# Out-projection A of a hybrid decoder step: loads issued from among the last gates, and a wait for each piece

## The chip, the cores and the metric

The kernel runs on one core of a Trainium2 chip. The metric is the device time of one execution in microseconds (us), as the median of several runs; lower is better. TensorE multiplies matrices, VectorE (DVE), ScalarE (ACT) and GpSimd (POOL) do the element-wise work, and SyncE (SP) issues the DMA transfers between device memory (DRAM) and the on-chip memory. TensorE's results go to PSUM banks, from which another engine evacuates them. Each engine takes its instructions in the order in which the program has them, and an instruction that waits holds up all behind it on that engine.

## The reference

One inference step of a decoder with two layers, for a prompt of 1024 positions (`x_prompt`) and 8 samples of one position each (`x_sample`), model width 1024, all in 32-bit floats. The part that the change touches is layer A, a gated-DeltaNet layer:

```python
def gdn_layer(x, conv_buf, s0, norm_g, w_in, conv_w, a_log, dt_bias, o_norm, w_out):
    proj = rmsnorm(x, norm_g) @ w_in
    qkv, gate, a, beta_logit = jnp.split(proj, [...], axis=-1)
    qkv, new_buf = causal_conv_silu(qkv, conv_buf, conv_w)
    ...
    o, s_fin = gated_delta_rule(q, k, v, g, beta, s0)
    o = rmsnorm(o, o_norm) * jax.nn.silu(gate)
    y = o.reshape(b, L, GDN_V_W) @ w_out
    return x + y, new_buf, s_fin
```

There are 8 heads of width 128; `gated_delta_rule` works through chunks of 64 positions, with a triangular inverse in each and a state that goes from chunk to chunk. The last matrix product, `o @ w_out` with a 1024 x 1024 matrix, plus the residual `x`, is out-projection A. Layer B (windowed attention with its own projections) follows and reads the sum.

## The kernel before, in words

Matrix operands are split into a high and a low part (`F32R` tiles; ScalarE copies the high part, VectorE subtracts it from the original for the low part), and a product is three matmuls: high by high, high by low, low by high (`PRS`, L1281). A weight or an input therefore goes from DRAM into a `raw` tile, and from there through one ScalarE cast and one VectorE subtraction into its high and low halves.

The kernel has three stretches. Up to about 81 us it loads and normalizes the input and does the first projections. Then comes the planned stage, which is about half of the span: the rest of layer A with most of its out-projection. Last comes the ordinary program (from L1392 on): the out-projection of the last two heads and of the samples, and layer B.

**The planner.** In the planned stage the work is written as generators (L599 to L1376) that yield operations instead of issuing them. The class `Order` (L478) keeps an estimated clock for each engine, the estimated time at which each part of each tile is ready, and a priority for each generator; `run` (L566) always emits the operation that can start first by these estimates. A generator can also yield `need(...)`, which lets it go on when other generators have set certain marks, and `get(...)`, which takes one of a counted set of slots (`od.slots`: PSUM tiles). `need` and `get` act at planning time only: they decide at which place of the order an operation is put. On the chip the engines wait for each other by semaphores on the data. All operations of the stage are issued from one line, L542, so in the profile they all carry that line. The constant `D0` (L53, used at L594) is the estimated time at which the decay inputs (`ghi`, `glo`, `eG` and others) are ready.

The generators that matter here:

- `proj_all` (L738), of the lowest priority (`FILL`, 9), yields the projections of layer A's input, head by head: k, q, v and gate of each head, in three groups of positions (384, 384, 264; `GRP`), 24 matmuls each. The gates of the last two heads (`late`) come at the very end (L763), group by group. Being of the lowest priority, these matmuls fill the gaps between the recurrence (`chains`), the inverses (`inverse`) and their preparation. The input that they read lies in the tiles `xg0` and `xg1` of the pool `wide` (tag `A`, two buffers) and `xg2` of the pool `thr`.
- `feed` and `split_all` (L690, L701) load and split the projection weights, through the two `raw` buffers of `raw0` (`RB[0]` is 2).
- `samples` (L1270) does the state update of the 8 samples: loads of the states (`ssm`), small matmuls (`sp`), updates (`up`) and stores.
- `out_all` (L1357) is called by `proj_all` when all gates are planned. It closes the pools of the gate weights and of the convolution inputs (`es2w`), opens on their place two more raw buffers (`raw1`) and the pool `p3a` for the input tiles, takes the two buffers of `wide` for the first two weight halves (`woa0` and `woa1`: 6 of 8 heads, 512 columns each) and starts `out_loads`. Then it waits for the mark `wa` (both halves split) and, for each of the 8 tiles of 128 positions, for the mark `ol` (the tile's inputs split), and yields 2 x 18 matmuls per tile. `out_evac` (L1349) adds the residual `hx` to the result and stores the sum to `hD`.
- `out_loads` (L1297) lists what is to be loaded: twelve weight pieces of one head by 512 columns, then for each tile two input pieces (`oD`, three heads each) and, between, the weight pieces of heads 6 and 7. Its `feed2` issues the loads; before the two input pieces of a tile it loads the residual tile `hx`. Tiles `ohl` (inputs) and `hx` have two buffers each, so the load of tile t waits in the plan for the store of tile t - 2.

Of the kernel before, what the change touches and what calls it, by code (L numbers as in the profile page):

```python
# [49 lines left out]
GA = 1  # L50


D0, PEM, VF, DP = 6000.0, 250.0, 1.0, 2000  # L53


@with_exitstack
def hybrid_step(
# [420 lines left out]
    class Order:  # L478
# [7 lines left out]
        def mark(self, *tok):  # L486
            self.toks.add(tok)
# [4 lines left out]
        def spawn(self, pri, gen):  # L492
            self.procs.append([pri, gen, None, 0.0])
# [105 lines left out]
    def need(*toks):  # L599
        yield ("need", toks)  # L600

    def get(name):
        yield ("get", name)
# [164 lines left out]

# [528 lines left out]
    def out_loads(wb, p3a):  # L1297

        src = w_out_a[0].rearrange("(k p) c -> p k c", p=P)
        todo = []  # L1300
        for j in range(2):
            c_ = ts(j, 512)
            todo += [("w", wa[j][:, 0, k:k + 1], wa[j][:, 1, k:k + 1], src[:, k:k + 1, c_]) for k in range(K1)]
        for t in range(NT):
            todo += [("o", t, k) for k in range(0, K1, 3)]
            if t in (2, 3):
                c_ = ts(t - 2, 512)
                todo += [("w", wb[:, 0, k - K1:k - K1 + 1, c_], wb[:, 1, k - K1:k - K1 + 1, c_], src[:, k:k + 1, c_])
                         for k in range(K1, KT)]
        nr = RB[0] + RB[1]  # L1310
        dsts = {}

        def feed2():
            for i, it in enumerate(todo):
                if i >= nr:
                    yield from need(("split2", i - nr))
                if it[0] == "o":
                    t, k = it[1:]
                    if k == 0:
                        yield from need(("o", K1 - 1))  # L1320
                        if t >= 2:
                            yield from need(("ot", t - 2))
                        ohl = p3a.tile([P, 2, K1, P], F32R, tag="ohl", name="ohl")
                        hx = p3a.tile([P, D], F32, tag="hx", name="hx")
                        ohx[t] = (hx, ohl)
                        yield dq.dma_start(out=hx, in_=x_prompt[0, ts(t, P), :])
                    hi, lo, sr = ohx[t][1][:, 0, k:k + 3], ohx[t][1][:, 1, k:k + 3], oD[:, k:k + 3, ts(t, P)]
                else:
                    hi, lo, sr = it[1:]
                _, nk, c = sr.shape  # L1330
                raw = raws[i % nr >= RB[0]].tile([P, 512], F32, tag="raw", name="raw")[:, :nk * c]
                raw = raw.rearrange("p (k c) -> p k c", c=c)
                yield dq.dma_start(out=raw, in_=sr)
                dsts[i] = (raw, hi, lo)
                mark("raw2", i)

        spawn(1.2, feed2())
        for i, it in enumerate(todo):
            yield from need(("raw2", i))
            raw, hi, lo = dsts.pop(i)  # L1340
            yield sq.copy(hi, raw)
            yield vq.tensor_tensor(out=lo, in0=raw, in1=hi.bitcast(F32), op=ALU.subtract)
            mark("split2", i)
            if it[0] == "o" and it[2]:
                mark("ol", it[1])
            elif i == 2 * K1 - 1:
                mark("wa")

    def out_evac(t, ci, ps):  # L1349
        hx, _ = ohx[t]  # L1350
# [2 lines left out]
        if ci:  # L1353
            yield dq.dma_start(out=hD[ts(t, P), :], in_=hx)
            mark("ot", t)

    def out_all():  # L1357
        es2w.close()
        raws.append(es3a.enter_context(tc.tile_pool(name="raw1", reuse_waits="tile", bufs=RB[1], side="right")))
        wa.extend(wide.tile([P, 2, K1, 512], F32R, tag="A", name=f"woa{i}") for i in range(2))  # L1360
        wb = thr.tile([P, 2, KT - K1, D], F32R, tag="B", name="woa2")
        wb_.append(wb)
        p3a = es3a.enter_context(tc.tile_pool(name="p3a", reuse_waits="tile", bufs=2, side="right"))
        spawn(1.2, out_loads(wb, p3a))
        spawn(8, out_gains(p3a))
        yield from need(("wa",))
        for t in range(NT):
            yield from need(("ol", t))
            _, ohl = ohx[t]
            for ci in range(2):  # L1370
                yield from get("pj")
                ps = pj.tile([P, 512], F32, tag="pj", name="pj")
                for i, (a, b) in enumerate(PRS):
                    for k in range(K1):
                        yield pm(ps, ohl[:, a, k, :], wa[ci][:, b, k, :], i + k == 0, i == 2 and k == K1 - 1)
                spawn(1.5, out_evac(t, ci, ps))  # L1376

    for i in range(2):
# [479 lines left out]
```

## Time and profile before

| | |
|---|---|
| median of 3 runs | 1325.34 us (1321.8 to 1326.71) |
| the profiled execution | 1322.79 us |
| its span, first to last instruction | 1321.1 us |
| mean granted TensorE clock | 0.977 of full speed |
| TensorE matmuls, busy share of the span | 94% |
| VectorE, ScalarE, GpSimd | 70%, 48%, 22% |
| data moved by DMA | 92.03 MB, mean 70 GB/s |

How to read it: the profile is of one execution. Times count from the start of the span. PE is TensorE's matmuls, PEld its weight loads, SPq the queue that issues DMA transfers. A busy share is an average over the whole span; a stage has to be read by itself. The granted clock is 1.00 at 2.4 GHz and 0.50 at 1.2 GHz, so a stretch between has been partly at each. In a timeline row stand the start, the duration, the engine, the line, the operation, the tile it writes and the tiles it reads (buffer numbers left out), and how many instructions are merged in the row; in square brackets the idle time before, and what ended it.

### The profile page before, as it was taken

How to read it: one execution, taken by the hardware profiler on the slowest of the kernel's cores; microseconds unless marked ns; L12 is line 12 of the kernel's file. 1: busy time of each engine (PE TensorE's matmuls, PEld its weight loads, DVE VectorE, ACT ScalarE, POOL GpSimd, SP SyncE). 2: the span in 40 equal slices, each digit the busy share in tenths (PEclk: the TensorE clock that was granted, in tenths of full speed). 3: DMA queues.
4: the chain of work that ended last, by engine and by line, in shares of the span. 5: the costliest groups of instructions: out<-in, count | busy, mean ns of one | idle time of the engine just before them, and what ended most of it. 6: DMA issues, size and time to landing. Idle time of an engine off the chain costs nothing.

```text
span 1321.1 us, 24330 instructions
## 1 busy us (share of the span) xinstructions
PE 1242.1 (94%) x8887; PEld 1121.0 (85%) x8887; DVE 923.8 (70%) x2656; ACT 634.8 (48%) x1812; POOL 286.5 (22%) x404
## 2 busy tenths in 40 slices
PE   4979999999999999989989898899999999999998
PEld 3979998899998989888967676788888888888898
DVE  7467778878978887788776329767686686777221
ACT  5235545645454454546352116455575476577100
POOL 1045243423323353243301103202011020000000
PEclk9989999999999999999979899999998999999999
DMA  7021101110221222111063657302011021102332
GB/s 236 1 80 34 35 17 51 34 52 18 67 65 53 78 65 85 34 35 35 25 194 118 211 186 221 88 17 64 4 43 39 4 55 29 49 1 69 127 96 72
DMA packets 131987, 92.03 MB, mean 70 GB/s; under 512 B 33880, under 2 KB 123712, under 8 KB 131808
## 3 DMA queue, kind: packets, MB, share of 16 engines
q1 hardware_dynamic: 131868, 90.48, 23.3%
q8 instruction: 70, 1.15, 0.4%
q14 instruction: 49, 0.40, 0.1%
HBM read 69.28 MB, written 23.25 MB: 70 GB/s over the span
## 4 chain that ended last, share of the span: by engine, by line
PE 69%; DVE 19%; ACT 5%; DMA 4%; issue 3%; SPq 0%; POOL 0%; DVEq 0%; ACTq 0%; POOLq 0%
PE pj L542 24%; PE pj L99 17%; PE ivt L542 4%; PE chB L542 3%; PE sps L99 3%; DVE co L542 2%; PE op L99 2%; PE chA L542 2%; PE ptp L1641 1%; DMA out_dram<-hx 1%; DVE wqkv L81 1%; DVE fu L542 1%; PE sp L542 1%; PE tq L1588 1%; DMA raw<-oD 1%
## 5 line engine op out<-in xcount | busy, mean ns | idle before, releaser
L542 PE MATMUL pj<-xg,whi 128*128 128x384 f32 (+1 forms) x1392 | 291.9, 336 | 0.0
L542 PEld LDWEIGHTS pj<-xg,whi 128*128 128x128 f32 x1392 | 223.2, 191 | 2.0 <-issue 1.5
L99 PE MATMUL pj<-wqkv,ng 128*128 128x384 f32 x768 | 154.2, 345 | 0.0
L542 PE MATMUL pj<-xg,wlo 128*128 128x384 f32 (+1 forms) x696 | 152.2, 335 | 0.0
L542 DVE SCALAR_TENSOR_TENSOR co<-ue,cvT,co 128x528 f32<-128x528 f32 x144 | 131.0, 916 | 12.3 <-ACT co L542 10.5
L99 PEld LDWEIGHTS pj<-wqkv,ng 128*128 128x128 f32 x768 | 132.6, 190 | 5.0 <-issue 4.6
L542 PEld LDWEIGHTS pj<-xg,wlo 128*128 128x128 f32 x696 | 112.3, 190 | 1.1 <-issue 0.5
L92 POOL TENSOR_TENSOR raw<-raw,gains 128x512 f32<-128x512 f32 x40 | 44.6, 1123 | 280.0 <-DMA raw<-in_w_in_b_dram 150.8
L99 PE MATMUL pj<-wob,oh 128*128 128x384 f32 (+1 forms) x576 | 98.1, 325 | 0.0
L99 PEld LDWEIGHTS pj<-wob,oh 128*128 128x128 f32 x576 | 90.7, 191 | 1.8 <-issue 1.5
L542 PE MATMUL pj<-woa,ohl 128*128 128x512 f32 x288 | 79.8, 428 | 6.5 <-ACT ohl L542 6.5
L542 PEld LDWEIGHTS pj<-woa,ohl 128*128 128x128 f32 x288 | 56.7, 204 | 21.6 <-ACT ohl L542 7.7
L542 ACT COPY ue<-pj 128x384 f32<-128x384 f32 (+1 forms) x88 | 32.2, 376 | 51.4 <-PE pj L542 43.6
L1819 DVE TENSOR_TENSOR hx<-hx,pj 128x384 f32<-128x384 f32 (+3 forms) x27 | 13.7, 508 | 59.0 <-PE pj L99 41.6
L542 POOL TENSOR_TENSOR ue<-ue,co 128x528 f32<-128x528 f32 x24 | 36.7, 1530 | 75.4 <-ACT ue L542 75.4
L542 DVE TENSOR_TENSOR wlo<-raw,whi 128x512 fp32r<-128x512 f32 x58 | 44.5, 770 | 9.9 <-ACT whi L542 9.4
L542 ACT ACTIVATE ue<-co 128x528 f32<-128x528 f32 x48 | 31.0, 645 | 31.3 <-DVE co L542 30.9
L542 ACT CAST whi<-raw 128x512 fp32r<-128x512 f32 x58 | 35.8, 619 | 19.6 <-PE pj L542 19.5
L99 PE MATMUL op<-pt,vsb 128*64 128x256 f32 x240 | 37.9, 396 | 0.7 <-DVE e L1625 0.5
L542 POOL TENSOR_TENSOR co<-co,ue 128x528 f32<-128x528 f32 x24 | 37.7, 1570 | 1.3
L542 ACT ACTIVATE qs<-chB,eG 128x128 f32<-128x128 f32 x56 | 20.5, 366 | 35.1 <-PE chB L542 34.5
L99 PE MATMUL sps<-kTh,qst 128*128 128x256 f32 (+1 forms) x144 | 36.9, 295 | 0.0
(906 smaller groups left out, 2950.4 us busy)
## 6 DMA issues: line engine op xcount, KB each, us to landing
raw<-in_w_in_a_dram SPq DMA_DIRECT2D x64, 256.0 KB
ssm<-in_state_ssm_dram SPq DMA_DIRECT2D x32, 256.0 KB
hD<-hx SPq DMA_DIRECT2D x16, 512.0 KB
raw<-in_w_in_b_dram SPq DMA_DIRECT2D x32, 256.0 KB
xt<-in_x_prompt_dram SPq DMA_DIRECT2D x8, 512.0 KB
out_dram<-ssm SPq DMA_DIRECT2D x16, 256.0 KB
raw<-in_w_out_a_dram SPq DMA_DIRECT2D x16, 256.0 KB
hx<-in_x_prompt_dram SPq DMA_DIRECT2D x8, 512.0 KB
```

The source lines that it names most:

```text
L81: V.tensor_tensor(out=lo, in0=raw, in1=hi.bitcast(F32), op=ALU.subtract)
L92: G.tensor_tensor(out=raw, in0=raw, in1=gain[:, k:k + n].unsqueeze(2).broadcast_to([P, n, c]), op=ALU.mult)
L99: PE.matmul(out, lhsT, rhs, start=start, stop=stop, skip_group_check=True)
L542: op.f(*op.a, **op.k)
L1588: PE.transpose(tq[:, ts(h, P)], qhl[:, h].rearrange("p a d -> p (a d)"), identr)
L1641: PE.transpose(pp[:, ts(h, P)], pr[h // 2][:, h % 2, ts(kt, P)], ident)
L1819: V.tensor_tensor(out=hx[:n, :cn], in0=hx[:n, :cn], in1=ps[:n, :cn], op=ALU.add)
```

## The change

- The first weight tile, `woa0`, is taken from `wide` as soon as the gates of the first group of positions are planned, and `out_loads` is started there; the second, `woa1`, after the gates of the second group. Before, both were taken after all gates.
- The list of loads is in another order: the six pieces of the first weight half, the two input pieces of tile 0, the six pieces of the second half, and then tile by tile as before.
- The loads of the second weight half and of the inputs wait (in the plan) for the mark `out`, set by `out_all` when the pools of the gate weights are closed. Up to there two raw buffers serve the loads, then four; they are counted as slots of `od`.
- The residual tile `hx` is loaded after the second input piece of its tile, before it was loaded ahead of the first.
- The marks `wa` and `ol` are gone. Each matmul needs (in the plan) its own weight piece and its own input piece.
- `D0` goes from 6000 to 12000 (ns).

```diff
-D0, PEM, VF, DP = 6000.0, 250.0, 1.0, 2000
+D0, PEM, VF, DP = 12000.0, 250.0, 1.0, 2000
...
         for gi in range(3):
             for i, (h, _) in enumerate(late):
                 yield from gate_group_a(h, gi, w_of[n + i])
+            if gi < 2:
+                wa.append(wide.tile([P, 2, K1, 512], F32R, tag="A", name=f"woa{gi}"))
+            if gi == 0:
+                spawn(1.2, out_loads())
...
-        todo = []
-        for j in range(2):
-            c_ = ts(j, 512)
-            todo += [("w", wa[j][:, 0, k:k + 1], wa[j][:, 1, k:k + 1], src[:, k:k + 1, c_]) for k in range(K1)]
-        for t in range(NT):
+        od.slots["raw"] = RB[0]
+        todo = [("w", 0, k, ts(0, 512)) for k in range(K1)] + [("o", 0, k) for k in range(0, K1, 3)]
+        todo += [("w", 1, k, ts(1, 512)) for k in range(K1)]
+        for t in range(1, NT):
             todo += [("o", t, k) for k in range(0, K1, 3)]
             if t in (2, 3):
...
         def feed2():
+            yield from need(("split", 2 * len(jobs) - 1))
             for i, it in enumerate(todo):
-                if i >= nr:
-                    yield from need(("split2", i - nr))
                 if it[0] == "o":
                     t, k = it[1:]
                     if k == 0:
-                        yield from need(("o", K1 - 1))
+                        yield from need(("o", K1 - 1), ("out",))
                         if t >= 2:
                             yield from need(("ot", t - 2))
...
-                        yield dq.dma_start(out=hx, in_=x_prompt[0, ts(t, P), :])
...
+                    j, k, c_ = it[1:]
+                    if j:
+                        yield from need(("out",))
...
+                yield from get("raw")
+                pool = rawfree.pop(0)
...
                 yield dq.dma_start(out=raw, in_=sr)
...
+                if it[0] == "o" and it[2]:
+                    yield dq.dma_start(out=ohx[it[1]][0], in_=x_prompt[0, ts(it[1], P), :])
...
     def out_all():
         es2w.close()
...
-        spawn(1.2, out_loads(wb, p3a))
-        spawn(8, out_gains(p3a))
-        yield from need(("wa",))
+        rawfree.extend([1] * RB[1])
+        od.slots["raw"] += RB[1]
+        mark("out")
+        spawn(8, out_gains(p3a[0]))
         for t in range(NT):
-            yield from need(("ol", t))
-            _, ohl = ohx[t]
             for ci in range(2):
                 yield from get("pj")
                 ps = pj.tile([P, 512], F32, tag="pj", name="pj")
                 for i, (a, b) in enumerate(PRS):
                     for k in range(K1):
-                        yield pm(ps, ohl[:, a, k, :], wa[ci][:, b, k, :], i + k == 0, i == 2 and k == K1 - 1)
+                        yield from need(("w", ci, k), ("o", t, 3 * (k // 3)))
+                        yield pm(ps, ohx[t][1][:, a, k, :], wa[ci][:, b, k, :], i + k == 0, i == 2 and k == K1 - 1)
```

## Rows read from the trace of the kernel before

**Rows 1.** Busy times of the page: us, share of the span, instructions.

```profile
PE 1242.1 (94%) x8887; PEld 1121.0 (85%) x8887; DVE 923.8 (70%) x2656; ACT 634.8 (48%) x1812; POOL 286.5 (22%) x404
```

**Rows 2.** Stretches: from:to length, busy us of PE PEld DVE ACT POOL, clock, DMA.

```profile
81.40:89.10 7.70, 1.99 (x6) 1.00 (x5) 6.88 (x9) 5.30 (x10) 4.58 (x5) 0.78 0.26 68
89.10:664.00 574.90, 554.76 (x4714) 520.09 (x4713) 467.17 (x997) 291.24 (x876) 213.69 (x309) 0.99 0.17 47
630.00:664.00 34.00, 32.95 (x299) 31.90 (x298) 24.53 (x68) 11.41 (x41) 8.42 (x14) 0.95 0.16 45
664.00:700.40 36.40, 29.17 (x193) 24.17 (x193) 27.74 (x76) 19.23 (x54) 3.75 (x5) 0.67 0.52 157
673.10:700.40 27.30, 21.92 (x100) 17.90 (x101) 21.41 (x59) 11.97 (x32) 3.03 (x3) 0.57 0.51 154
735.70:765.70 30.00, 29.70 (x111) 22.25 (x112) 11.04 (x21) 5.18 (x12) 4.75 (x7) 0.91 0.75 234
774.30:777.10 2.80, 0.06 (x1) 0.00 (x0) 0.69 (x1) 0.51 (x2) 0.00 (x0) 1.00 0.52 202
777.10:787.20 10.10, 10.05 (x36) 8.00 (x37) 1.74 (x3) 0.49 (x2) 0.00 (x0) 0.83 0.01 5
787.20:830.00 42.80, 37.82 (x183) 26.31 (x182) 38.17 (x116) 28.61 (x49) 11.41 (x13) 1.00 0.69 206
```

**Rows 3.** Timeline of TensorE's matmuls, at the start, the hand-over and the out-projection.

```profile
87.50 0.80 PE L542 MATMUL dps<-gm,mgtr 128*128 128x512 f32 x1 [5.46 <-POOL gm L542]
...
110.99 3.07 PE L542 MATMUL pj<-xg,whi 128*128 128x384 f32 x16
...
663.25 0.49 PE L542 MATMUL pj<-xg,whi 128*128 128x264 f32 x2
...
693.19 2.05 PE L542 MATMUL pj<-woa,ohl 128*128 128x512 f32 x4
...
735.76 11.04 PE L542 MATMUL pj<-woa,ohl 128*128 128x512 f32 x36 [3.50 <-ACT ohl L542]
...
765.70 8.66 PE L542 MATMUL pj<-woa,ohl 128*128 128x512 f32 x36 [0.23 <-ACT ohl L542]
```

**Rows 4.** Timeline of the DMA queue (SP), hand-over and out-projection.

```profile
660.61 1.88 SPq L542 DMA_DIRECT2D raw<-in_w_out_a_dram  x4
...
672.03 11.22 SPq L542 DMA_DIRECT2D raw<-in_w_out_a_dram  x7
...
729.05 0.39 SPq L542 DMA_DIRECT2D out_dram<-ssm  x1
...
766.22 0.32 SPq L542 DMA_DIRECT2D hD<-hx  x1
...
770.08 0.33 SPq L542 DMA_DIRECT2D hx<-in_x_prompt_dram  x1
770.51 1.48 SPq L542 DMA_DIRECT2D raw<-oD  x2
```

**Rows 5.** Timeline of ScalarE (ACT).

```profile
81.90 1.13 ACT L542 CAST whi<-raw 128x512 fp32r<-128x512 f32 x2
...
85.78 0.57 ACT L542 ACTIVATE dt<-dps 128x512 f32<-128x512 f32 x1
...
632.23 0.49 ACT L542 ACTIVATE ogs<-pj 128x384 f32<-128x384 f32 x1
...
665.40 0.62 ACT L542 CAST woa<-raw 128x512 fp32r<-128x512 f32 x1
...
755.56 0.71 ACT L1415 CAST ohl<-ogs 128x256 fp32r<-128x256 f32 x2
```

**Rows 6.** Timeline of VectorE (DVE).

```profile
107.22 0.69 DVE L542 TENSOR_TENSOR m<-nps,dt 128x512 f32<-128x512 f32 x1
...
687.18 0.69 DVE L542 TENSOR_TENSOR woa<-raw,woa 128x512 fp32r<-128x512 f32 x1 [0.56 <-ACT woa L542]
...
727.69 0.75 DVE L542 SCALAR_TENSOR_TENSOR ogs<-otp,ogain,ogs 128x512 f32<-128x512 f32 x1
```

More of the change, by code (lines that the diff above doesn't have):

```diff
@@ L1295, in out_gains, with out_loads @@
         free("gen")
-    def out_loads(wb, p3a):
+    rawfree = [0] * RB[0]
+    def out_loads():
         src = w_out_a[0].rearrange("(k p) c -> p k c", p=P)
-        todo = []
-        for j in range(2):
-            c_ = ts(j, 512)
-            todo += [("w", wa[j][:, 0, k:k + 1], wa[j][:, 1, k:k + 1], src[:, k:k + 1, c_]) for k in range(K1)]
-        for t in range(NT):
+        od.slots["raw"] = RB[0]
+        todo = [("w", 0, k, ts(0, 512)) for k in range(K1)] + [("o", 0, k) for k in range(0, K1, 3)]
+        todo += [("w", 1, k, ts(1, 512)) for k in range(K1)]
+        for t in range(1, NT):
             todo += [("o", t, k) for k in range(0, K1, 3)]
             if t in (2, 3):
[L1307 to L1311, printed above, removed]
+                todo += [("w", 2, k, ts(t - 2, 512)) for k in range(K1, KT)]
+        pieces = {}
         def feed2():
+            yield from need(("split", 2 * len(jobs) - 1))
             for i, it in enumerate(todo):
-                if i >= nr:
-                    yield from need(("split2", i - nr))
                 if it[0] == "o":
@@ L1319, in feed2 @@
                     if k == 0:
-                        yield from need(("o", K1 - 1))
+                        yield from need(("o", K1 - 1), ("out",))
                         if t >= 2:
                             yield from need(("ot", t - 2))
-                        ohl = p3a.tile([P, 2, K1, P], F32R, tag="ohl", name="ohl")
-                        hx = p3a.tile([P, D], F32, tag="hx", name="hx")
-                        ohx[t] = (hx, ohl)
-                        yield dq.dma_start(out=hx, in_=x_prompt[0, ts(t, P), :])
+                        ohx[t] = (p3a[0].tile([P, D], F32, tag="hx", name="hx"),
+                                  p3a[0].tile([P, 2, K1, P], F32R, tag="ohl", name="ohl"))
                     hi, lo, sr = ohx[t][1][:, 0, k:k + 3], ohx[t][1][:, 1, k:k + 3], oD[:, k:k + 3, ts(t, P)]
                 else:
-                    hi, lo, sr = it[1:]
+                    j, k, c_ = it[1:]
+                    if j:
+                        yield from need(("out",))
+                    w_, k_ = (wa[j], k) if j < 2 else (wb_[0][:, :, :, c_], k - K1)
+                    hi, lo, sr = w_[:, 0, k_:k_ + 1], w_[:, 1, k_:k_ + 1], src[:, k:k + 1, c_]
                 _, nk, c = sr.shape
-                raw = raws[i % nr >= RB[0]].tile([P, 512], F32, tag="raw", name="raw")[:, :nk * c]
-                raw = raw.rearrange("p (k c) -> p k c", c=c)
+                yield from get("raw")
+                pool = rawfree.pop(0)
+                raw = raws[pool].tile([P, 512], F32, tag="raw", name="raw")[:, :nk * c].rearrange("p (k c) -> p k c", c=c)
                 yield dq.dma_start(out=raw, in_=sr)
-                dsts[i] = (raw, hi, lo)
+                pieces[i] = (pool, raw, hi, lo)
                 mark("raw2", i)
+                if it[0] == "o" and it[2]:
+                    yield dq.dma_start(out=ohx[it[1]][0], in_=x_prompt[0, ts(it[1], P), :])
         spawn(1.2, feed2())
@@ L1339, in out_loads @@
             yield from need(("raw2", i))
-            raw, hi, lo = dsts.pop(i)
+            pool, raw, hi, lo = pieces.pop(i)
             yield sq.copy(hi, raw)
             yield vq.tensor_tensor(out=lo, in0=raw, in1=hi.bitcast(F32), op=ALU.subtract)
[L1343 to L1347, printed above, removed]
+            rawfree.append(pool)
+            free("raw")
+            mark(*it[:3])
     def out_evac(t, ci, ps):
@@ L1355, in out_evac @@
             mark("ot", t)
+    p3a = []
     def out_all():
@@ L1359, in out_all @@
         raws.append(es3a.enter_context(tc.tile_pool(name="raw1", reuse_waits="tile", bufs=RB[1], side="right")))
[L1360 to L1363, printed above, removed]
-        spawn(1.2, out_loads(wb, p3a))
-        spawn(8, out_gains(p3a))
-        yield from need(("wa",))
+        wb_.append(thr.tile([P, 2, KT - K1, D], F32R, tag="B", name="woa2"))
+        p3a.append(es3a.enter_context(tc.tile_pool(name="p3a", reuse_waits="tile", bufs=2, side="right")))
+        rawfree.extend([1] * RB[1])
+        od.slots["raw"] += RB[1]
+        mark("out")
+        spawn(8, out_gains(p3a[0]))
         for t in range(NT):
-            yield from need(("ol", t))
-            _, ohl = ohx[t]
             for ci in range(2):
```

## The prediction

> **What bounds the kernel now.** I read the page's busy times first, then a table of stretches, then the timelines of TensorE, of the DMA queue (SP) and of the two copying engines around the change. TensorE is busy for 94% of the span [rows 1]. In the planned stage it idles 20 us of the 575 us from 89.1 to 664, at a granted clock of 0.99 [rows 2]: there the amount of matmul work sets the end, and the planner fills the gaps with projections. So what I look for is time in which TensorE had nothing to fill with, or ran at its lower level.
>
> There are three such places. The largest is the hand-over. The last gate matmuls are issued at 663.25 and the first matmul of out-projection A at 693.19 [rows 3]. Between them only the recurrence of the last head and the sample update are left. From 664 to 700.4 TensorE is busy 29.17 of 36.4 us. From 673.1 to 700.4 the granted clock is 0.57, so about 23.5 of 27.3 us ran at 1.2 GHz and not at 2.4 [rows 2]. In those 30 us the kernel waits for twelve weight pieces and the input pieces behind them: SP issues the weight loads from 660.61 until about 683 [rows 4], the first cast is at 665.40 [rows 5] and the last low half is made at 687.18 [rows 6].
>
> The second place is inside the out-projection: a wait of 3.50 us [rows 3] and one of about 2.8 us [rows 2] for an input tile. The third is the start of the planned stage: TensorE waits 5.46 us for a masked decay tile of POOL [rows 3], and the clock is 0.78 on average [rows 2].
>
> **The change, part by part.** The sum is made against the profiled execution, 1322.79 us (span 1321.1), which is 2.55 us below the median of 1325.34. No matmul, cast, subtraction or load is added or removed; all are moved.
>
> *A, the hand-over.* Only the six pieces of the first weight half start among the gates; second half and inputs still wait for the gates' end, because their buffers lie where the gate weights were. What can be had at most is the idle time, 36.4 - 29.17 = 7.2 us, and half of what TensorE did at the low clock: 23.5 / 27.3 of the 21.92 busy us [rows 2], 18.9 / 2 = 9.4 us. Together 16.6 us. What stays: after the gates, input pieces have to come. Before, the first piece took from 660.61 until its cast at 665.40, so the first matmul can stand at about 666, 2.3 us after the gates. Further pieces come at the pace of before: twelve from 660.61 to 687.87, 2.27 us each [rows 4 to 6]. The second weight half is complete with the eighth piece, at 679, and the next input tile with the tenth, at 683. Up to there the out-projection can fill with its first tile, 36 matmuls or 8.66 us [rows 3]; afterwards it never lacks work. TensorE takes its queue in order, so a matmul put too early holds up the recurrence as well; I charge two piece times, 4.5 us. A = 16.6 - 2.3 - 4.5 = 10 us. Ends: a gain of 16.6 us, and a loss of 5 us if the pieces hold up the queue by two more times than I charge and nothing is won. I take 10: the pace of the pieces is a row, and the first tile covers half of the 17 us until the next.
>
> *The moved loads and splits.* Six loads enter SP's queue among the last gates, after those of the first 384 positions (the last is evacuated at 632.23 [rows 5]). Only two raw buffers are free then, so SP stands before every further piece until a split is done; the sample-state loads queue behind it, and the sample matmuls wait for those. Four buffers gave 2.27 us a piece; for two I allow 4.5 us, 27 us for six, from 632 to 659: in time. For the delayed state loads I charge 1 us (0 to 4). VectorE gets six subtractions of 0.69 us [rows 6], 4.1 us in a stretch where it is busy 24.53 of 34 us [rows 2]. That can delay the last head by 4 us. Its last output is written at 727.69 [rows 6] and first needed at 755.56 [rows 5]; even with the out-projection 15 us earlier the cover holds. ScalarE has more room, 11.41 of 34 [rows 2]. Cost on the path: 0.
>
> *B, the order of an input tile's loads.* Before, the residual tile is loaded first; its buffer has to be stored before that, so SP stands: store issued at 766.22, residual load at 770.08, input pieces from 770.51 [rows 4]. TensorE then idles from 774.3 to 777.1 and has a clock of 0.83 until 787.2 [rows 2]. Now the input pieces go ahead of the residual load, 3.8 us earlier. The wait of 2.8 us goes, with the 0.23 us before 765.70 [rows 3] and the low clock behind it, 0.17 x 10.1 = 1.7 us: 4.7 us. The wait of 3.50 us comes from elsewhere: SP issues a sample-state store at 729.05 and only then the tile's loads [rows 4]; these stores stay, and I count none of it. The residual tile comes later, but only the evacuation needs it, and the two PSUM banks cover one tile, 8.66 us. I take 4. Ends: 0 (the pieces wait behind state traffic instead), and 4.7 + 3.50 + 0.09 x 30 = 10.9 us, with the clock of 0.91 from 735.7 on [rows 2].
>
> *C, the planner's due time of the decays, from 6 to 12 us.* It changes the order of all that is planned. On the chip TensorE stood 5.46 us before a decay matmul at 87.50 [rows 3], with projections behind it whose first weights were cast from 81.90 on [rows 5]. With the decays planned later, the projections come first. I count one group of 24 matmuls of 384 columns (16 took 3.07 us [rows 3]), 4 us, before a mask of POOL holds TensorE up again. Ends: the 5.46 us and some 2.5 us of low clock, 8 us; and a loss of 6 us, the amount by which the decays are put off. What covers that: the first decay was finished by ScalarE at 85.78 [rows 5] and used at 107.22 [rows 6].
>
> What follows the out-projection (787.2 to 830: TensorE busy 37.82 of 42.8 [rows 2]) moves along. Sum: 10 + 4 + 4 - 1 = 17 us, 1322.8 - 17 = 1305.8; with half of the 2.55 us to the median, **1307 us**.
>
> One rule of the Trainium skill speaks against A. The trace shows that the sparse stage of 36 us had a clock of 0.67 and the packed 575 us before it 0.99 [rows 2]. The page “TensorE: Matmul & The Clock Gate”, section “A second HAM failure mode: psum-queue depth-cycling”, says that short but frequent idle times between groups of matmuls make the clock swing and cost throughput. By that, waiting piece by piece would keep the low clock here; the trace agrees for the sparse stage, and shows nothing for one that is half filled.
>
> **The rivals.**
> *The clock stays low at the hand-over.* The pieces come 2.27 us apart, and TensorE stands between them. Then only some 4 us of the idle 7.2 are gained for A: 1322.8 - 11 + 1.3 = 1313. The same comes out if the early loads stand behind the state loads in SP until 660, so that the change hardly does what it says. For it: 0.67 now. Against: the first tile fills 8.66 us. Chance 0.08.
> *The gain is given back in the loads.* The out-projection starts earlier, but from the third tile on each needs a store, a residual load and two input pieces through one SP queue that also carries the sample states. If each of six tiles loses 2 us to that, 12 us of the 17 are gone: 1319. For it: both waits of before are of this kind. Against: from 735.7 to 765.7 TensorE is busy 29.70 of 30 [rows 2]. Chance 0.15.
> *Everything is larger*: the upper ends of A and B with C as taken give 1322.8 - 16.6 - 10.9 - 4 = 1291. Chance 0.10.
> *Slower: the new due time makes a worse order in every head.* Place: TensorE's queue from 89.1 to 664, where decays, inverse and recurrence are then planned later than the chip has them ready, or earlier, and TensorE stands for each in order. Idle time there is now 20 us for eight heads, 2.5 us each. Beyond 2.1 us more per head the 17 us are gone; at 5 us more the time is 1322.8 + 40 - 17 = 1346. Against: the first decay has 21 us of cover, and the later ones wait for data of their own head, not for this number. Chance 0.07.
>
> **How the numbers follow.** My forecast has 0.60, with 1296 to 1317. About 0.5% (6.6 us) is what a measurement of this kernel can tell from no change. Faster by more: forecast, larger gain and low clock, 0.60 + 0.10 + 0.08 = 0.78; within: 0.15; slower: 0.07. The range takes in the low clock and half of the loads' case, and leaves out the slower case and the largest gains: 1292 to 1320.
>
> **What would show it.** A: first out-projection matmul between 664 and 670, not at 693, and a clock over 0.9 from 664 to 700. If the weight casts begin only after 660, the early start failed. B: no TensorE wait over 1 us for an input tile in the last three tiles, input pieces issued right behind the store. C: no 5 us wait for a decay tile, first projection matmul near 83. The prediction is wrong if TensorE's idle time between 89 and 664 rises by more than 10 us, or if the out-projection starts early and yet ends near its old time.

## The result, and the profile after

The changed kernel takes 1302.09 us (median of 4 runs, 1298.07 to 1304.35), the kernel before 1323.57 in the same comparison: ratio 0.9844, 95% interval 0.9814 to 0.9873. It is faster by 1.6%. The profiled execution took 1303.65 us, its span is 1302.0.

The page's busy line of the changed kernel, beside [rows 1]:

```profile
PE 1227.2 (94%) x8887; PEld 1112.0 (85%) x8887; DVE 926.3 (71%) x2656; ACT 634.8 (49%) x1812; POOL 288.4 (22%) x404
```

The same matmuls take TensorE 14.9 us less: that much of the gain is clock. The stretches say where (columns as in [rows 2]; the last four rows are stretches of the kernel **before** that were not shown yet: layer B, the rest of the out-projection, the hand-over, and the planned out-projection behind it):

```profile
82.40:656.40 574.00, 551.75 (x4713) 518.12 (x4714) 483.85 (x1012) 300.37 (x893) 219.73 (x315) 0.99 0.18 50
656.40:700.00 43.60, 42.48 (x320) 35.53 (x316) 33.06 (x97) 19.27 (x57) 4.34 (x5) 1.00 0.63 193
700.00:749.80 49.80, 49.80 (x220) 38.45 (x218) 21.14 (x46) 8.82 (x24) 6.25 (x6) 1.00 0.61 193
749.80:800.40 50.60, 39.41 (x170) 27.18 (x170) 35.13 (x113) 25.14 (x45) 13.46 (x18) 0.90 0.71 223
808.10:1157.30 349.20, 338.37 (x2142) 302.20 (x2141) 246.48 (x1010) 201.30 (x610) 37.27 (x35) 0.98 0.13 33
...
834.20:1179.10 344.90, 335.08 (x2142) 299.20 (x2141) 245.43 (x1009) 201.29 (x610) 36.17 (x35) 0.99 0.13 33
787.40:826.60 39.20, 35.66 (x168) 24.58 (x166) 35.43 (x106) 25.21 (x44) 11.41 (x13) 1.00 0.72 214
663.70:700.40 36.70, 29.47 (x202) 24.47 (x200) 27.74 (x76) 19.46 (x54) 3.75 (x5) 0.67 0.52 158
700.40:787.40 87.00, 80.12 (x338) 61.43 (x338) 35.20 (x81) 13.60 (x37) 8.91 (x11) 0.94 0.58 185
```

From 656.4 to 749.8 TensorE idles 1.1 us and has its full clock. Before, the same work went from 663.7 to 787.4, with 14.1 us idle (7.2 up to 700.4, 6.9 behind it) and a clock of 0.67 and 0.94. The row from 749.8 is the surprise: the rest of the out-projection (heads 6 and 7, and the samples; in both kernels the ordinary program behind the planned one) takes 50.6 us instead of 39.2, with the clock at 0.90 instead of 1.00.

TensorE's timeline of the changed kernel (start, duration, instructions, and in brackets the idle time before and what ended it): the rows that answer to [rows 3], and the two waits in that stretch:

```profile
82.47 1.68 PE L542 MATMUL pj<-xg,whi 128*128 128x384 f32 x8 [0.99 <-ACT whi L542]
...
92.52 0.50 PE L542 MATMUL dps<-gm,mgtr 128*128 128x512 f32 x1 [1.30 <-POOL gm L542]
...
659.73 0.48 PE L542 MATMUL pj<-woa,ohl 128*128 128x512 f32 x1
...
757.12 3.78 PE L99 MATMUL pj<-woa,ohl 128*128 128x512 f32 x8 [5.78 <-DVE ohl L1420]
764.27 8.32 PE L99 MATMUL pj<-woa,ohl 128*128 128x512 f32 x28 [3.38 <-DVE hx L1433]
```

SP's queue of the changed kernel, beside [rows 4]: the early weight loads, one tile in the middle, and the end of the planned part:

```profile
616.69 19.65 SPq L542 DMA_DIRECT2D raw<-in_w_out_a_dram  x6
...
714.02 0.33 SPq L542 DMA_DIRECT2D hD<-hx  x1
714.44 1.30 SPq L542 DMA_DIRECT2D raw<-oD  x2
...
717.06 0.45 SPq L542 DMA_DIRECT2D hx<-in_x_prompt_dram  x1
...
750.53 0.34 SPq L542 DMA_DIRECT2D hD<-hx  x1
750.98 0.38 SPq L542 DMA_DIRECT2D ssm<-in_state_ssm_dram  x1
751.44 0.86 SPq L542 DMA_DIRECT2D out_dram<-ssm  x1
752.40 1.96 SPq L90 DMA_DIRECT2D raw<-in_w_in_b_dram  x3
756.59 0.38 SPq L542 DMA_DIRECT2D out_dram<-ssm  x1
757.03 0.50 SPq L90 DMA_DIRECT2D raw<-in_w_in_b_dram  x1
757.62 2.09 SPq L1412 DMA_DIRECT2D hx<-hD  x4
```

The six early weight pieces and the input pieces right behind the store are there, as foretold. The end of the list is new. The last state load of the sample update is issued at 750.98, behind the last planned store, and the four residual tiles of the next stage (L1412) at 757.62, behind all planned stores. Before, SP issued those four loads (L1408) at 761.71 and 766.59, some 20 us ahead of the planned end at 787.4:

```profile
761.71 0.89 SPq L1408 DMA_DIRECT2D hx<-hD  x2
...
766.59 1.23 SPq L1408 DMA_DIRECT2D hx<-hD  x2
...
775.12 13.34 SPq L542 DMA_DIRECT2D hD<-hx  x2
```

So the order of SP's queue in the built program is not that of the source, where these loads stand behind the whole planned stage. What gives them their place was not looked into.

As a ledger, after against before, in us from the span's start: planned out-projection ends at 749.8, not 787.4 (-37.6); the rest ends at 800.4, not 826.6 (-26.1); layer B's output projection begins at 1157.3, not 1179.1 (-21.8); the span ends at 1302.0, not 1321.1 (-19.1). Half of what was won at the out-projection was given back behind it. The experiments ask what won it, and what took it back.

### The profile page after: what moved, and what is told of

Same layout as the page of the kernel before. It is cut to its first block, busy times and chain, and to the rows that moved or that the text cites. A ratio compares the mean times of both kernels' runs of the same rounds, so it can differ in the third digit from the quotient of the medians.

```text
span 1302.0 us, 24333 instructions
## 1 busy us (share of the span) xinstructions
PE 1227.2 (94%) x8887; PEld 1112.0 (85%) x8887; DVE 926.3 (71%) x2656; ACT 634.8 (49%) x1812; POOL 288.4 (22%) x404
## 4 chain that ended last, share of the span: by engine, by line
PE 70%; DVE 17%; ACT 4%; DMA 4%; issue 3%; POOL 2%; SPq 0%; DVEq 0%; ACTq 0%; POOLq 0%
PE pj L542 24%; PE pj L99 17%; PE ivt L542 4%; DVE co L542 3%; PE sps L99 3%; PE chB L542 3%; PE op L99 2%; PE chA L542 2%; PE ptp L1645 1%; DMA out_dram<-hx 1%; DVE wqkv L81 1%; PE sp L542 1%; PE nps L542 1%; PE tq L1592 1%; PE psab L99 1%
## 5 line engine op out<-in xcount | busy, mean ns | idle before, releaser
L542 DVE SCALAR_TENSOR_TENSOR co<-ue,cvT,co 128x528 f32<-128x528 f32 x144 | 134.6, 941 | 16.1 <-ACT co L542 14.5
L542 PE MATMUL pj<-woa,ohl 128*128 128x512 f32 x288 | 76.1, 406 | 0.0
L542 PEld LDWEIGHTS pj<-woa,ohl 128*128 128x128 f32 x288 | 51.7, 188 | 11.6 <-issue 1.5
L1823 DVE TENSOR_TENSOR hx<-hx,pj 128x384 f32<-128x384 f32 (+3 forms) x27 | 13.7, 508 | 60.5 <-PE pj L99 45.9
L542 POOL TENSOR_TENSOR ue<-ue,co 128x528 f32<-128x528 f32 x24 | 33.9, 1412 | 71.1 <-ACT ue L542 71.1
L542 DVE TENSOR_TENSOR wlo<-raw,whi 128x512 fp32r<-128x512 f32 x58 | 43.6, 758 | 7.7 <-ACT whi L542 7.6
L99 PE MATMUL op<-pt,vsb 128*64 128x256 f32 x240 | 37.9, 396 | 0.9 <-DVE e L1629 0.8
L1536 ACT ACTIVATE jk<-pj 128x320 f32<-128x320 f32 x32 | 13.9, 435 | 50.4 <-PE pj L99 50.4
L99 PE MATMUL pj<-woa,ohl 128*128 128x512 f32 x96 | 27.7, 442 | 11.2 <-DVE ohl L1420 5.8
```

Of the source, the lines that this page charges most:

```text
L99: PE.matmul(out, lhsT, rhs, start=start, stop=stop, skip_group_check=True)
L542: op.f(*op.a, **op.k)
L1536: S.activation(jk[:n], src, AF.Square)
L1823: V.tensor_tensor(out=hx[:n, :cn], in0=hx[:n, :cn], in1=ps[:n, :cn], op=ALU.add)
```

## The experiments

Below, "planned end" is the end of the planned out-projection's last matmul, and "the phase behind it" runs from there to the last matmul of the rest of it. Ratios are against the kernel before, run on the same chip.

**One part alone, or undone.** Four kernels: the due time alone, the due time undone, the early start undone, the wait for the own piece undone.

```
e1 (kernel before)   -D0, PEM, VF, DP = 6000.0, ...
                     +D0, PEM, VF, DP = 12000.0, ...
e2 (changed kernel)  -D0, PEM, VF, DP = 12000.0, ...
                     +D0, PEM, VF, DP = 6000.0, ...
e3 (changed kernel)  -            if gi == 0:
                     -                spawn(1.2, out_loads())
                     ...
                          mark("out")
                     +    spawn(1.2, out_loads())
e4 (changed kernel)  +        yield from need(("w", 0, K1 - 1), ("w", 1, K1 - 1))
                              for t in range(NT):
                     +            yield from need(("o", t, 3))
                     -                        yield from need(("w", ci, k), ("o", t, 3 * (k // 3)))
```

> The kernel before with the due time of the decays at 12 us and nothing else changed. Theory (the due time is worth the start of the planned stage alone): the first planned projection matmul near 83 us instead of 89.15, the last gate matmul near 657 instead of 663.7, the hand-over as before (first out-projection matmul 29 us after the last gate matmul, granted clock near 0.6 between), the end 6 to 7 us earlier: about 1316 us, ratio near 0.995. Rival (the new due time changes the order of the whole stage, and that makes most of the 21 us): 1310 us or less. Second rival (the 7 us are lost again in waits behind): over 1320 us.

Measured: 1318.96 us, ratio 0.9966 (0.9944 to 0.9988). First projection matmul at 81.94, planned end at 779.1, 8.3 us earlier; the phase behind it 38.9 us. In the profiled execution the lead is 8.7 us at the end of that phase and 3.8 at the end of the span. So the due time is worth 8 us at the out-projection and some 4.5 at the end. The last gate matmul did not move (663.6), against the forecast of 657: with the due time of 12 us, 4793 matmuls are done by then instead of 4709. The hand-over has that many fewer left to do; its clock was 0.81, where it was 0.67 before.

> The changed kernel with the due time of the decays back at 6 us. Theory (the parts add up): the 5.5 us wait for a decay tile is back at about 87 us, the last gate matmul near 663 instead of 656.4, everything behind it 6 to 7 us later, about 1309 us (changed kernel: 1302). Rival (the start's gain is eaten anyway by the wait for the sample update behind the out-projection): 1304 us or less.

Measured: 1309.72 us, ratio 0.9909 (0.9875 to 0.9943), as the theory says, but not in the way it says. The wait of 5.45 us is back at 87.27, yet the last gate matmul comes at 651.3, not at 663 (4587 matmuls are done by then, 4713 in the changed kernel), and the planned end is only 3.1 us later (752.9). The last sample-update matmul comes at 765, and the phase behind ends at 813.9 instead of 800.4. TensorE's timeline of e2:

```profile
761.27 0.79 PE L542 MATMUL up<-db,kl 24*128 24x512 f32 x1 [6.18 <-DVE ssm L542]
764.26 0.79 PE L542 MATMUL up<-db,kl 24*128 24x512 f32 x1 [2.20 <-DVE ssm L542]
772.51 3.78 PE L99 MATMUL pj<-woa,ohl 128*128 128x512 f32 x8 [5.45 <-DVE ohl L1420]
```

The out-projection was done and TensorE stood for the sample update (`up`). That was the first sight of the new bound.

> The changed kernel with the out-projection's loads begun only after the last gate matmul; the order of the pieces and the wait for each piece stay. Theory (the wait for the own piece gives the out-projection work early enough; the early start adds only what the first pieces need): the first out-projection matmul 6 to 12 us after the last gate matmul instead of 3.4, TensorE idle 5 to 10 us longer there and some of it at the lower clock, the planned out-projection ends 8 to 15 us later than 749.8; of that about 6 us are hidden, since TensorE waits 5.8 us for the sample update at 757 in the changed kernel: the end at 1304 to 1311 us. Rival (the early start is the whole hand-over gain): first out-projection matmul 25 us or more after the last gate matmul, granted clock near 0.6, end at 1318 us or later.

Measured: 1301.94 us, ratio 0.9852 (0.9817 to 0.9886): the same as the changed kernel. The forecast was 1304 to 1311. First out-projection matmul at 672.8, 9.5 us after the last gate; planned end at 763.4, 13.7 us later than with the early start; the phase behind it 38.5 us instead of 50.6. The stretches of e3, hand-over and phase:

```profile
663.30:700.00 36.70, 29.58 (x177) 23.38 (x177) 28.51 (x87) 15.96 (x45) 3.43 (x4) 0.91 0.52 163
...
763.30:801.80 38.50, 35.65 (x169) 24.77 (x167) 34.52 (x106) 25.00 (x44) 11.40 (x13) 1.00 0.77 236
```

The early start wins 13.7 us at the planned end, and some 12 of it are lost in the phase behind: the out-projection is over at 801.8 here and at 800.4 in the changed kernel.

> The changed kernel with the out-projection begun only when both weight halves are split, and a tile begun only when both of its input pieces are; the early start and the order of the pieces stay. Theory (the wait for the own piece is the larger part of the hand-over's gain): first out-projection matmul near 675 us instead of 659.7, TensorE idle 6 to 10 us between 656 and 676 and the granted clock near 0.6 for some 20 us, the planned out-projection ends near 765, the end at 1310 to 1316 us. Rival (the early start alone brings most of it): first matmul before 668, the end at 1305 us or earlier.

Measured: 1310.68 us, ratio 0.9903 (0.9869 to 0.9937): the wait for the own piece is worth some 8 us at the median, though the two intervals just touch. First matmul at 677.11, planned end at 760.0. The first two stretches of e4 behind its gates:

```profile
656.10:677.10 21.00, 17.25 (x157) 15.46 (x154) 14.94 (x36) 10.83 (x30) 0.71 (x2) 0.68 0.54 172
677.10:700.00 22.90, 22.90 (x123) 19.69 (x123) 14.24 (x55) 6.97 (x25) 2.36 (x3) 0.92 0.36 112
```

TensorE idles 3.75 us (6 to 10 were forecast) where the changed kernel idles 1.1, and the clock is 0.68: most of the loss is clock.

**The order of an input tile's loads.** e5 puts the residual load first again.

```
+                        yield dq.dma_start(out=ohx[t][0], in_=x_prompt[0, ts(t, P), :])
-                if it[0] == "o" and it[2]:
-                    yield dq.dma_start(out=ohx[it[1]][0], in_=x_prompt[0, ts(it[1], P), :])
```

> The changed kernel with the residual load again ahead of a tile's input pieces. Theory (the order is worth what the prediction put on it): the SP queue stands some 4 us before each residual load from the third tile on, TensorE waits 2 to 3 us for an input tile in several of the last six tiles, the planned out-projection ends at 755 to 762 us instead of 749.8, the end moves by the part of it that is not hidden behind the sample update, 0 to 6 us: 1302 to 1308. Rival (the order matters nothing, the raw buffers and the piece-wise wait cover it): planned out-projection ends within 2 us of 749.8 and the end within 2 us of 1302.

Measured: 1295.84 us, ratio 0.9787 (0.9749 to 0.9826), the fastest of all; both forecasts missed. TensorE does wait for an input tile, as the theory says, and the planned end is 9 us later; the phase and layer B are what differ. TensorE's timeline and stretches of e5:

```profile
719.20 6.43 PE L542 MATMUL pj<-woa,ohl 128*128 128x512 f32 x20 [3.67 <-ACT ohl L542]
740.57 6.32 PE L542 MATMUL pj<-woa,ohl 128*128 128x512 f32 x26 [1.16 <-ACT ohl L542]
```

```profile
758.70:797.70 39.00, 35.76 (x169) 24.77 (x167) 35.01 (x106) 25.18 (x44) 11.43 (x13) 1.00 0.75 232
806.40:1149.30 342.90, 333.17 (x2141) 297.56 (x2140) 244.82 (x1009) 201.73 (x612) 35.93 (x34) 1.00 0.13 34
```

Its out-projection is over at 797.7, 2.7 us before that of the changed kernel. The other 5.5 us of the profiled difference lie behind, 6.3 us in layer B, which does the same work at a clock of 1.00 instead of 0.98. That it is faster than the changed kernel at all is not quite settled: the intervals overlap.

**What takes the gain back: first guess.** The waits at 757 and 764 name VectorE. Behind them stood the late state load, and a zeroed tile (`ohs`) that GpSimd makes behind four multiplications of layer B's weights; ScalarE waits 24.7 us for it. In VectorE's timeline of the changed kernel they are these rows:

```profile
755.88 0.69 DVE L542 TENSOR_TENSOR ssm<-ssm,up 128x512 f32<-128x512 f32 x1 [4.77 <-POOL ssm L542]
...
763.30 0.23 DVE L1415 TENSOR_TENSOR ohs<-ogm,ohs 128x64 fp32r<-128x64 f32 x1 [5.91 <-ACT ohs L1414]
```

e6 lets VectorE make the tile, e7 issues the late state loads from GpSimd's queue, e8 does both.

```
e6  -        zero_r(hs, scr)
    -        zero_r(ohs, scr)
    +        V.memset(scr, 0.0)
    +        V.tensor_copy(ohs, scr)
    +        G.tensor_copy(hs, scr)
e7  +    gdq = Later("D", G)
    -                return dq.dma_start(out=svs[hh], in_=...)
    +                return (gdq if h0 else dq).dma_start(out=svs[hh], in_=...)
```

> The changed kernel with the zeroed sample tile (ohs) made by VectorE instead of GpSimd, so that it does not stand behind the first multiplications of layer B's weights. Theory (two waits stand at the end of the planned stage: first the sample update, then this tile): ScalarE's wait for the zeroed tile ends near 758 instead of 763, the second TensorE wait (3.4 us at 764.3) goes, the first (5.8 us at 757.1) stays, the phase behind the planned out-projection takes 45 to 47 us instead of 50.3, the end at 1297 to 1299 us. Rival (the tile is not what holds the phase up; transfers or the clock are): no change within 2 us of 1302.

> The changed kernel with the second reading of the sample states of heads 4 to 7 issued by GpSimd's queue instead of SP's; the order of the matmuls is the same. Theory (the last state load is late because it stands in SP's queue behind a store that waits for an evacuation; with it the sample update sets the end of the phase): the last update lands near 751 instead of 756.6, the 5.8 us wait at 757 shrinks to 1 us or less, GpSimd's order behind it changes as well and the 3.4 us wait shrinks, the phase behind the planned out-projection takes about 40 us instead of 50.3 and the end comes at 1291 to 1295 us. Rival (the transfers themselves are short of bandwidth in this stretch, whichever queue issues them): the loads take as much longer, phase of 48 us or more, end within 3 us of 1302.

> Both: the zeroed sample tile by VectorE, and the second reading of the sample states of heads 4 to 7 by GpSimd's queue. Theory: neither wait is left, the phase behind the planned out-projection takes 38.5 to 40 us, as it does where the out-projection sets the end (39.4 before), the end at 1290 to 1293 us. Rival (something else bounds the phase, such as the loads of layer B's weights): 45 us or more and an end above 1297.

Measured: e6 1302.5 us, ratio 0.9836 (0.9795 to 0.9877); e7 1299.23, 0.98 (0.9751 to 0.9849); e8 1304.02, 0.9856 (0.9813 to 0.99). None differs from the changed kernel, and the phase stayed at 50.7 to 51.4 us. The guess falls. VectorE's timeline of e8 shows why (its line numbers are one or two higher):

```profile
754.17 0.69 DVE L543 TENSOR_TENSOR ssm<-ssm,up 128x512 f32<-128x512 f32 x1 [1.49 <-POOL ssm L543]
...
756.44 0.23 DVE L1417 TENSOR_TENSOR ohs<-ogm,ohs 128x64 fp32r<-128x64 f32 x1
763.93 1.28 DVE L1435 TENSOR_TENSOR hx<-hx,pj 128x512 f32<-128x512 f32 x2 [7.26 <-DMA hx<-hD]
```

The last sample update and the zeroed tile are 1.7 and 6.9 us earlier than in the changed kernel (755.88 and 763.30), and VectorE waits 7.26 us for the residual tile instead. On TensorE the first wait is 2.77 us instead of 5.78, the second 6.44 instead of 3.38: their sum is nearly the same. The two named causes had stood in front of a third that ends at the same time: the four residual loads at the tail of SP's queue.

**Second guess: the residual loads.** In SP's order of every kernel the picture is the same. Where at least one of the four loads stands ahead of the last planned store (before, e1, e3, e5, and e10 and e11 below), the phase takes 38 to 39 us; where all stand behind it (changed kernel, e2, e4, e6 to e8), 46.8 us or more. That a late planned end alone makes the phase short is ruled out by e4 and e10: their planned ends are at 760.0 and 760.3, their phases 46.8 and 39.2 us; e4 issues the four loads at 763.45, behind its last planned store at 760.77, and e10 issues them so:

```profile
747.82 0.46 SPq L1413 DMA_DIRECT2D hx<-hD  x1
...
752.99 1.79 SPq L1413 DMA_DIRECT2D hx<-hD  x3
761.00 0.32 SPq L542 DMA_DIRECT2D hD<-hx  x1
```

In the other kernels the loads come behind the sample update's last stores, so e9 gives its second reading four buffers instead of two; e10 adds the residual load first, e11 also undoes the early start; e12 is e9 with the four loads in GpSimd's queue.

```
e9   +        if h0:
     +            yield from need(("vt", 2 * H - 1))
     -                svs[hh] = gd.tile(B4, F32, tag="ssm", name="ssm")
     +                svs[hh] = gd.tile(B4, F32, tag="vt", name="ssm", bufs=NB) if h0 else gd.tile(B4, F32, tag="ssm", name="ssm")
e12  -            DMA.dma_start(out=hx[:n], in_=... hD[ts(t, P), :])
     +            (G if t < 4 else DMA).dma_start(out=hx[:n], in_=... hD[ts(t, P), :])
```

> The changed kernel with four buffers instead of two for the second reading of the sample states of heads 4 to 7 (the ring of the value tiles is used again). In the runs so far the phase behind the planned out-projection took 38.4 to 39.4 us where the last sample update came 7 us or more before the planned end, and 46 to 51 us where it came with or after it; the first residual loads of that phase stand behind the last state store in SP's queue. Theory (the end of the sample update, not the zeroed tile or the queue of its loads, starts that phase): the last update comes one tile (some 8 us) before the planned end, which stays within 3 us of 750; the wait of 5.8 us for the low half of heads 6 and 7 goes, a wait for the residual tile of some 3 us may stay, since those loads still stand behind the last planned store; phase 40 to 45 us, end at 1291 to 1297 us. Rival (the phase is bounded by the loads of layer B's weights and the residual tiles themselves): phase 48 us or more, end above 1299.

Measured: 1301.83 us, ratio 0.9838 (0.9781 to 0.9895). Planned end at 751.7, the wait for the low half is gone, but the loads still stand behind the last store, and the wait for them is larger than forecast, 6.24 us; phase 46.8 us. No gain at the median.

> Four state buffers, and the residual load ahead of a tile's input pieces. With the residual load first alone the planned out-projection ended 9 us later than in the changed kernel (758.8) and the time was 1295.8 us. Theory (the order of an input tile's loads helped only by letting the sample update end before the out-projection): with the update early anyway the residual load first costs its waits for an input tile (3.7 and 1.2 us) and brings nothing more: planned end 756 to 762, phase 38 to 40 us, end at 1293 to 1299 us, the same as with two buffers or up to 4 us slower than four buffers with the input pieces first. Rival (residual first is better of itself): 1291 us or less, and faster than the four buffers alone.

> Four state buffers, residual load first, and the out-projection's loads begun only after the last gate matmul. The late start alone left the time where it was (1301.9 us), with the planned end 13.7 us later and the phase behind it 12 us shorter. Theory (the early start's gain was hidden behind the sample update): with the update out of the way the late start shows: planned end at 764 to 772 us, phase 38 to 40, end at 1303 to 1309 us, 8 to 13 us behind the same kernel with the early start. Rival (the early start is worth nothing, since the gates it moves aside have to be done anyway): within 3 us of the kernel with the early start.

Measured: e10 1299.38 us, ratio 0.9821 (0.9774 to 0.9868); e11 1311.23, 0.9924 (0.9899 to 0.995). In both, SP issues two or more of the residual loads ahead of the last planned store and the phase is 39.2 and 37.9 us. Here the early start shows: the out-projection is over at 799.5 with it and at 813.3 without, and the time differs by 12 us. As for the order of the loads, e9 and e10 are not told apart. But e11 is slower than e3 (ratio 0.9852, 0.9817 to 0.9886), and both lack the early start: its planned end is at 775.4, that of e3 at 763.4. Beside more buffers, e11 has the residual load first. So at the end the early start and the order of a tile's loads stand in for each other: a kernel with one of them (e3; e5 and e10) is about as fast as the changed kernel, which has both, and e11, which has neither, is slower. (The share of the four buffers in e11 was not measured apart.)

> The kernel with four state buffers, and the first four residual loads of the phase behind the planned out-projection issued by GpSimd's queue instead of SP's. With four state buffers alone TensorE waited 6.2 us for a residual tile at 761.35, the four loads having been issued at 755.16, behind the last planned store and two weight loads; in all runs so far the phase took 38 to 39.4 us where at least one of these loads stands ahead of the last planned store in SP's queue, and 46 to 51 us where all stand behind it. Theory (the place of these loads in SP's queue sets the start of the phase): issued by 750 us, landed by 755, no TensorE wait over 1.5 us, phase 38.5 to 41 us, the end 7 to 10 us earlier than with four state buffers alone (profiled 1294.3, median 1301.8): 1285 to 1295 us. Rival (the tiles lie in memory that the sample update still holds, so the loads have to wait for the last state store, which SP issues at 752.8): issued at 755 or later whatever the queue, phase 45 to 48 us, no gain.

Measured: 1298.68 us, ratio 0.9827 (0.9795 to 0.9858), against e9 no difference that is sure; phase 44.8 us, TensorE's wait 4.42 instead of 6.24. GpSimd's timeline of e12:

```profile
745.63 0.74 POOL L1414 DMA_DIRECT2D hx<-hD  x1
...
752.88 0.53 POOL L1414 DMA_DIRECT2D hx<-hD  x1 [5.87 <-DMA out_dram<-ssm]
...
759.98 0.53 POOL L1414 DMA_DIRECT2D hx<-hD  x1 [6.19 <-DVE ohl L1422]
```

Theory and rival share it. The first load was held by its place alone: it goes out 9.5 us earlier than in e9. The second waits for a state store, the third for VectorE's low half of heads 6 and 7: most likely their tiles take over memory that is still in use, which was not tried by itself.

None of these kernels won the lost time back. In the changed kernel, e3, e5 to e10 and e12 the out-projection is over between 797.7 and 803.6 us, whether its planned part ends at 749.8 or at 763.4. That TensorE waits for the residual tiles is shown, and that the phase is short where their loads are issued early. That their place in SP's queue is the cause is not shown: no run moves these loads alone within that queue, and in the other queue (e12) the first two left 9.5 and some 2 us earlier than in e9, the last two some 3 us later.

## Why the prediction was right, and where its steps were not

The time came out 5 us under the forecast and well inside the range, by two errors that cancel, and that they cancel is luck: the parts won 37.6 us at the planned end where 18 were counted (A, B and C), and "what follows moves along" was wrong by 18.5 us (37.6 - 19.1). Of these, 11.5 us lie in the phase behind the planned end, and 7.0 in layer B and behind it, where the time also differs from one execution to the next (last section). Undone one at a time, the parts take from the planned end 13.7 us (the early start, e3), 10.2 (the wait for the own piece, e4), 9.1 (the order of a tile's loads, e5) and 3.1 (the due time, e2), some 36 of the 37.6 together.

- **A, the hand-over: undersized.** The ceiling of 16.6 us was right, the 6.8 us taken off it were not. I put 2.3 us for the first piece and 4.5 us for matmuls that hold up the recurrence; idle and clock loss from 656.4 to 700 are 1.1 us in all, so some 15.5 us were won where 10 were counted. What I had left out: with the out-projection to fill with, 80 matmuls fewer stand before the last gate matmul than with the same due time and no early start (4713 in the changed kernel, 4793 in e1 and e3). Those are left for the hand-over. The first matmul at 659.7 was earlier than the 664 to 670 foretold, but the last gate matmul was 7.3 us earlier too; it stands 3.4 us behind that.
- **The moved loads: right.** They cost nothing that can be seen: TensorE idles 22.3 us in the planned part, 21.9 in e1, which has the same due time and no early loads. The six loads went out from 616.69 to 636.3, sooner than the 632 to 659 foretold.
- **B, the order of a tile's loads: right in kind, undersized, and gone at the end.** The wait of 2.8 us went, and so did the one of 3.50, of which I had counted none; undone, two waits come back and the planned end is 9 us later (e5), twice the 4 I took and inside its ends. But in e5 three of the four residual loads stand ahead of the last planned store, and the out-projection is over no later than in the changed kernel.
- **C, the due time: undersized.** I counted 4 us; alone it is 8.3 at the planned end (e1), about my upper end of 8, and 4.5 at the end (1.6 to 7.4 by the interval). Beside the other parts it is 3.1 at the planned end (e2). The wait of 5.46 us is 1.30 now, and the first projection matmul is at 82.47, as foretold. The idle time in the planned part is 22.3 us (20 before), so the slower rival is out.
- **What follows: the step that failed.** I took the stretch behind the out-projection as a block that moves. It has a chain of its own: last sample update, last stores, residual loads, in that order in SP's queue. Before, it was over some 20 us ahead of the out-projection and so in no wait. That chain moved forward by 8 us only: the last of the four residual loads left at 767.8 before and at 759.7 now. Pulled 38 us forward, the out-projection overtook it, and the phase went from 39.2 to 50.6 us: idle 3.5 to 11.2 us, and the clock 1.00 to 0.90. This is the rival "the gain is given back in the loads" in kind, but at another place: I had put it into the tiles of the out-projection, where nothing was lost.
- **The clock rival: did not come.** The granted clock stayed at 1.00 through the hand-over, with 1.1 us idle in 43.6 and no wait over 0.75 us. In e4 it is 0.86 from 660 to 665, where TensorE idles 2.8 of 5.0 us, then 0.50 up to 677, and 1.00 again from 683: one fall and one rise. The page “TensorE: Matmul & The Clock Gate” of the Trainium skill, section “A second HAM failure mode: psum-queue depth-cycling”, tells of a kernel in which frequent short idle times make the clock swing. This case agrees in part: the lower level follows idle time in e4, but it does not swing there, and e3, with 7.1 us idle in 36.7, has 0.91.

## What to carry to other kernels

When a stage is to be shortened, list every chain that ends near it, with the time at which each is over, and not only the one that sets the end: what may be gained in full is the distance to the second. Loads of the next stage that stand behind the last store of this one in an in-order queue are such a chain, even if no wait shows before (here TensorE's wait for them is shown; whether their place in the queue or memory still in use held them stays open). And a wait named in a profile may stand in front of another that ends at the same time: e8 took away the causes of two of them, and a wait of the same sum stood in their place.

## What the runs showed of the hardware that was not expected

Layer B has the same matmuls in every kernel, and took 341.4 (e2) to 349.5 us (e7) in the profiled executions. Its granted clock goes with it: 0.98 in the changed kernel (349.2 us), 0.99 before (344.9), and 1.00 in e5 (342.9) and in e9:

```profile
806.10:1147.80 341.70, 332.09 (x2142) 296.27 (x2141) 244.86 (x1009) 201.42 (x610) 36.59 (x35) 1.00 0.13 33
```

In one place of layer B (1066.21 in the changed kernel) TensorE waits for VectorE. The wait is 1.98 us in the changed kernel and 1.71 in e6, and in both the next 10 us have a clock of 0.66; it is 1.54 in e5, 1.59 before, 1.85 in e2 and 1.86 in e9, and there the clock stays at 1.00. So its length alone does not decide. At the place before it (970.75 in the changed kernel), waits of 2.33 to 2.88 us (before, changed kernel, e5, e6) are followed by the lower level, and waits of 1.59 and 1.71 us (e2, e9) are not. What decides stays open; the time and the mean clock differ together from one execution to the next (e9: 1294.29 us at 0.990, 1305.42 at 0.984). Most likely the 4.3 us that the changed kernel loses in layer B are of this kind, and so is much of e5's lead; no run shows it.
